# First attention of a two-layer step: score tiles of 768 keys over two PSUM banks, three banks for transposed weights

## The chip, the cores and the metric

One core of a Trainium2 chip runs the whole program. Its engines issue their own instructions in a fixed order: PE (TensorE, matmuls and transposes, with its weight loads listed as PEld), DVE (VectorE), ACT (ScalarE), POOL (GpSimd) and SP (SyncE, which here issues DMAs). The metric is the time of one execution on the device in microseconds; lower is better.

## The reference

One inference step of a backbone of two layers, on 256 prompt tokens and 1024 sample tokens of width 1024, with 512 cached keys for the samples. Layer 0 has a convolution branch and a differential attention; layer 1 has two grouped-query attentions. The attention of layer 0 has 4 heads of two score maps each:

```python
def diff_attend(q, k, v, lam):
    s = jnp.einsum('bqhcd,bkhcd->bhcqk', q, k).astype(F32) * (q.shape[-1] ** -0.5)
    p = jax.nn.softmax(s, axis=-1)
    w = p[:, :, 0] - lam * p[:, :, 1]
    return jnp.einsum('bhqk,bkhv->bqhv', w.astype(v.dtype), v)
```

A sample token attends to 512 cached and 1024 own keys, 1536 in all; a prompt token to the 256 prompt keys. The outcome is normalized, multiplied with a gate, and goes into one output projection together with the convolution branch.

## The kernel before

The kernel keeps float32 results by writing an operand as a high and a low part of a faster 32-bit format. A product is then two or three matmuls that add up in PSUM. PSUM has 8 banks of 128 x 512 float32.

The work of a layer runs in stages: input projection, attention, output projection. In the attention of layer 0, `l0_attn`, the tokens are taken in groups of two row blocks of 128; group 0 is the prompt, groups 1 to 4 the samples. For each of 4 heads and each group, `stage_a` loads the queries (L661, tile `qs`, three of them) and goes through the two row blocks j and the two maps c, with a row of tiles for each pair (j, c):

- Scores: for every 512 keys a PSUM tile `S` takes two matmuls (L777), the high and the low part of the queries in one. A sample row has three such tiles. The pool has three `S` buffers of one bank.
- `row_softmax` (L385 to L398): DVE reads an `S` tile, writes its negative to `E` in SBUF and takes the running minimum into a column of `mm` (L394). The second and third reduce of a row start from the minimum of the one before, so each depends on it. When all of a row is there, ACT takes the exponential of all 1536 columns with its sum (L397).
- After both maps of a block: a reciprocal (L784), a factor (L785), and `E0 += w * E1`, the first 1024 columns on DVE (L787), the last 512 on POOL (L789, L790).

`stage_b` (L668 to L733) then multiplies the weights with the values. For every 256 keys it transposes four blocks of 128 x 128 on PE into a PSUM tile `wt` (L690); four buffers of one bank. That tile is copied out in one of three ways: ACT copies, DVE casts the high part (L371), POOL subtracts for the low part (L372); or ACT does both reads (L374, L375) and POOL subtracts (L376); or ACT copies alone (L696). The products go into the one `pv` bank: three matmuls a chunk (L677 to L679), or one in float32 (L684). At the end of a group ACT copies `pv` out (L710), PE transposes it back into a further `wt` buffer, named `wt_ot` (L717), from which ACT takes squares (L718) and DVE, after a few small steps and a power on POOL (L95), the scaled output `oy` (L724). SP stores it. The tiles of the next stage's first two preparations use `wt` buffers as well.

So the banks are 3 for `S`, 4 for `wt` and 1 for `pv`.

Steps of `stage_b` of one group are put between the rows of the next by a small queue (`BQueue`, L37 to L74) that hands out so many chunks a row. In what order the instructions finally stand on each engine is set by the framework's list scheduler, which the program is opened with (`schedule_with_timeline_sim=True`, L1547); tile pools with their numbers of buffers bound it. On the chip an engine works down its order: behind an instruction that waits, all that follows waits too.

In `phase_attn` (L1274 to L1295) the pools are made, from the numbers in `pb` (L1269). Layer 1 (scores at L1217) shares `row_softmax` and `phase_attn`.

Of the kernel before, what the change touches and what calls it, by code (L numbers as in the profile page):

```python
# [10 lines left out]
F32 = mybir.dt.float32  # L11
# [21 lines left out]
def f32(ap):  # L33
    return ap.bitcast(F32)
# [42 lines left out]
class K:  # L77
# [586 lines left out]
    def l0_attn(self, at, small, pre, sps, wps, pvps, freed, early):  # L664
        nc, a = self.nc, self.a
# [71 lines left out]
        for h in range(4):  # L737
            kd = nxt
            if h == 3:
                freed()  # L740
            nxt = None
            vf = at.tile([128, NT + 4, 128], F32, tag="v", bufs=2, name=f"v{h}")
            nc.sync.dma_start(vf[:, 0:NT], self.V0[h].rearrange("t p c -> p t c"))
            nc.sync.dma_start(vf[:, NT : NT + 4], a["cbv"][h])
            vs = None
            nr = sum(2 for m in self.modes0 if m not in ("a", "d"))
            if nr:
                vs = at.tile([128, 2, nr, 128], F32R, tag="vs", bufs=2, name=f"vs{h}")
                nc.scalar.copy(vs[:, 0], vf[:, 2 : 2 + nr])
                nc.gpsimd.tensor_tensor(vs[:, 1], vf[:, 2 : 2 + nr], f32(vs[:, 0]), ALU.subtract)  # L750
            gzt = at.tile([128, NT, 128], F32, tag="gzt", bufs=2, name=f"gzt{h}")
            nc.sync.dma_start(gzt, self.GZ0[h].rearrange("t p c -> p t c"))

            def stage_a(h, g, kd, vf, vs, gzt):

                tiles = (2 * g, 2 * g + 1)
                sample = g > 0
                kofs = 256 if sample else 0
                nkc = 1536 if sample else 256
                qs = qs1 if (h, g) == (0, 1) else self.l0_query(h, g, at, 3)  # L760
                sc = small.tile([128, 2, 2], F32, tag="sc", bufs=4, name=f"sc{h}_{g}")
                W = []
                for j in range(2):
                    E = []
                    for c in range(2):
                        nmx = f"{h}_{g}_{j}_{c}"
                        q = qs[:, :, c, j * 128 : j * 128 + 128]
                        if sample:
                            e = at.tile([128, 1536], F32, tag=f"E{c}", bufs=(4 if c == 0 else 3), name=f"E{nmx}")
                        else:  # L770
                            e = at.tile([128, 256], F32, tag="Ep", bufs=4, name=f"E{nmx}")
                        parts = []
                        for o in range(0, nkc, 512):
                            n = min(512, nkc - o)
                            S = sps(f"{nmx}_{o}")[:, :n]
                            for hl in range(2):
                                nc.tensor.matmul(S, q[:, hl], kd[:, c, kofs + o : kofs + o + n], start=(hl == 0), stop=(hl == 1))  # L777
                            parts.append((S, o))
                        m = small.tile([128, 4], F32, tag="mm", bufs=8, name=f"mm{nmx}")
                        self.row_softmax(parts, e, sc[:, c, j : j + 1], m)  # L780
                        E.append(e)
                        yield
                    w = small.tile([128, 2], F32, tag="wc", bufs=4, name=f"wc{h}_{g}_{j}")
                    nc.vector.reciprocal(w[:, 0:1], sc[:, 1, j : j + 1])  # L784
                    nc.vector.scalar_tensor_tensor(w[:, 1:2], sc[:, 0, j : j + 1], self.nlam, w[:, 0:1], ALU.mult, ALU.mult)  # L785
                    sp = self.wsp if sample else nkc
                    nc.vector.scalar_tensor_tensor(E[0][:, :sp], E[1][:, :sp], w[:, 1:2], E[0][:, :sp], ALU.mult, ALU.add)  # L787
                    if sp < nkc:
                        nc.gpsimd.tensor_scalar(E[1][:, sp:nkc], E[1][:, sp:nkc], w[:, 1:2], 0.0, ALU.mult, ALU.add)  # L789
                        nc.gpsimd.tensor_tensor(E[0][:, sp:nkc], E[0][:, sp:nkc], E[1][:, sp:nkc], ALU.add)  # L790
                    W.append(E[0])
                bq.put(stage_b(h, tiles, W, sc, nkc // 128, (vf, vs, 2 if sample else 0), gzt), nkc // 256)

            prompt = stage_a(h, 0, kd, vf, vs, gzt)
            for g in range(1, 5):
                for i, _ in enumerate(stage_a(h, g, kd, vf, vs, gzt)):
                    bq.step(4 - i)
                    if (g, i) == (2, 2) and h < 3:
                        nxt = self.l0_keys(h + 1, *((pool, 1) if h == 1 else (at, 2)))
                    if g == self.gp:  # L800
                        next(prompt, None)
                if g == self.gp:
                    for _ in prompt:
                        pass
# [427 lines left out]
def build(tc, a):  # L1232
    nc = tc.nc
    k = K(tc, a)
    with ExitStack() as ctx:
# [30 lines left out]
        def pool(c, name, bufs=1, **kw):  # L1266
            return c.enter_context(tc.tile_pool(name=name, bufs=bufs, **T, **kw))

        pb = (dict(S=3, wt=4), dict(S=3, wt=4))  # L1269

        def right(name):
            return tc.alloc_tile_pool(name=name, bufs=1, side="right", **T)

        def phase_attn(l, fn, pre):  # L1274
            out = []

            def freed():
                while pre[0]:
                    pre[0].pop().release()
                wp = right(f"wop{l}")  # L1280
                out.extend([wp, [k.wo_chunk(l, j, wp) for j in range(k.npre[l])], []])

            def early(t, ps):
                out[2].append(k.prep(l, t, out[0], lambda nm: out[0].tile([128, D], F32, tag="ac2", bufs=1, name=nm), ps))

            with ExitStack() as c:
                at = pool(c, f"at{l}")
                small = pool(c, f"sa{l}", 2)
                psp = pool(c, f"pa{l}", space=PSUM)
                fn(at, small, (pre[0][-1], *pre[1:]),  # L1290
                   lambda nm: psp.tile([128, 512], F32, tag="S", bufs=pb[l]["S"], name=f"S_{nm}"),
                   lambda nm: psp.tile([128, 512], F32, tag="wt", bufs=pb[l]["wt"], name=f"wt_{nm}"),
                   lambda nm: psp.tile([128, 512], F32, tag="pv", bufs=1, name=f"pv_{nm}"),
                   freed, early)
            return out  # L1295
# [13 lines left out]
        with ExitStack() as c1:  # L1309
# [5 lines left out]
            psp = pool(c1, "ps0", space=PSUM)  # L1315
# [85 lines left out]
            k.hlb = 1  # L1401
            k.l0_in(ws, raw, wp, cxp, p1, small, acc, pst, mod, freed0)
        wo = phase_attn(0, k.l0_attn, pre)
        with ExitStack() as c1:
            hpa = pool(c1, "hpa")
            k.use_mod()
            with ExitStack() as c2:
# [13 lines left out]
                psp = pool(c1, "ps1", space=PSUM)  # L1421
# [23 lines left out]
            k.hlb = 2  # L1445
            k.l1_in(ws, (kvw[0], k.nkv), raw, wp, p1, small, acc1, pst1, k.mod_vec(((1, 2),), cr, raw, wp, small, psm1, cst, [k.vec1]), freed1)
        wo = phase_attn(1, k.l1_attn, pre)
        with ExitStack() as c1:
            psp = pool(c1, "ps2", space=PSUM)
# [111 lines left out]
```

## Time and profile before

| | before |
|---|---|
| median of 3 runs | 1828.53 us |
| lowest and highest | 1826.63, 1828.82 us |
| profiled execution, its own time | 1829.44 us |
| its span in the trace | 1827.6 us |
| around the span | 1.84 us |
| mean granted clock of PE | 0.983 |
| PE busy, of the span | 1728.4 us (95%) |
| DVE busy | 1246.9 us (68%) |
| ACT busy | 974.5 us (53%) |
| POOL busy | 780.3 us (43%) |
| first sample reduce of layer 0's attention | at 529.93 us |
| last one | at 783.56 us |

The profiled execution is 0.91 us above the median. Shares of the whole span mix stages with different limits, so the attention of layer 0 is read in windows of its own. In a row of groups, the columns are: line, engine, operation, what is written and read, shapes, the count, then busy time, the mean of one in ns, and the idle time of the engine ahead of these instructions with what ended most of it. In a row of the timeline, they are the start, the duration, engine, line and operation, and in brackets the idle time ahead of it. A reduce at L394 shows up as two records, the reduce and the read of its accumulator.

### The profile page before, as it was taken

The page shows a single profiled execution, that of the slowest core. Times are in us where ns is not written, and L with a number is a line of the kernel's source. Part 1 is how long each engine was busy: PE and PEld are TensorE (multiplying, and loading weights), DVE is VectorE, ACT ScalarE, POOL GpSimd, SP SyncE. Part 2 cuts the span into 40 slices and gives each one's busy share as a digit, 9 for nine tenths or more (in the row PEclk, how much of TensorE's full clock was granted, in tenths as well). Part 3 has the DMA queues.
Part 4 walks back from the last instruction along what each step waited for, and adds up shares of the span by engine and source line. Part 5 has one row for each costly group of instructions (what it writes and reads, how often), then busy time and mean ns, then how long its engine had stood idle before and what let it go on. Part 6 is the DMA issues. An engine that isn't in the chain of part 4 may idle for free. (4 is left out here: it accounts for less than half of the span.)

```text
span 1827.6 us, 28287 instructions
## 1 busy us (share of the span) xinstructions
PE 1728.4 (95%) x9434; PEld 1419.7 (78%) x9434; DVE 1246.9 (68%) x2975; ACT 974.5 (53%) x2040; POOL 780.3 (43%) x696
## 2 busy tenths in 40 slices
PE   6999999999859999899999999998999999999998
PEld 2787888988747777778887778876888888878886
DVE  6657545674779999945576672117999999999322
ACT  6432234444337777653344543217888788898311
POOL 2322022222547787663237873203344344454332
PEclk9999999999969999999999999999999999999999
DMA  8467478785764433144246346254013114141441
GB/s 292 167 164 209 155 189 208 191 225 134 230 192 107 125 104 96 44 140 160 75 158 194 139 122 167 75 137 101 24 41 90 36 38 110 54 146 58 158 171 55
DMA packets 220086, 241.24 MB, mean 132 GB/s; under 512 B 72128, under 2 KB 154464, under 8 KB 219684
## 3 DMA queue, kind: packets, MB, share of 16 engines
q1 hardware_dynamic: 207284, 233.53, 43.2%
q0 software_dynamic: 1792, 3.15, 1.0%
q10 hardware_dynamic: 10864, 2.75, 0.8%
q8 instruction: 75, 1.23, 0.3%
q14 instruction: 71, 0.58, 0.1%
HBM read 169.08 MB, written 70.28 MB: 131 GB/s over the span
## 5 line engine op out<-in xcount | busy, mean ns | idle before, releaser
L397 ACT ACTIVATE E<-E,mm 128x1536 f32<-128x1536 f32 (+3 forms) x240 | 293.2, 1226 | 78.1 <-DVE E L394 63.6
L270 POOL TENSOR_TENSOR w_w<-raw_w,w_w 128x512 fp32r<-128x512 f32 x88 | 118.6, 1358 | 256.2 <-ACT w_w L269 242.4
L1217 PE MATMUL S<-k1d,q1s 128*128 128x512 f32 (+1 forms) x704 | 204.7, 391 | 2.5 <-DVE E L394 0.9
L372 POOL TENSOR_TENSOR el<-ef,eh 128x512 fp32r<-128x512 f32 x96 | 123.9, 1291 | 190.9 <-DVE eh L371 185.9
L394 DVE TENSOR_SCALAR_CACHE_REDUCE E<-S,mm 128x512 f32<-128x512 f32 x256 | 189.8, 743 | 10.7 <-PE S L777 3.7
L1147 PE MATMUL wt_et<-ident,E 128*128 128x128 f32 x1264 | 187.6, 273 | 4.9 <-ACT ef L370 4.4
L1147 PEld LDWEIGHTS wt_et<-ident,E 128*128 128x128 f32 x1264 | 154.7, 140 | 41.3 <-ACT ef L370 4.8
L777 PE MATMUL S<-kd,qs 128*128 128x512 f32 (+1 forms) x416 | 134.2, 433 | 30.4 <-DVE E L394 25.3
L368 DVE TENSOR_TENSOR el<-wt_et,eh 128x512 fp32r<-128x512 f32 x220 | 146.4, 681 | 11.8 <-ACT eh L367 11.3
L1217 PEld LDWEIGHTS S<-k1d,q1s 128*128 128x128 f32 x704 | 119.6, 190 | 27.9 <-DVE E L394 11.8
L1142 PE MATMUL pv_pv<-el,v 128*128 128x512 f32 x316 | 139.3, 441 | 0.4 <-POOL el L372 0.2
L318 PE MATMUL acc_g<-w_w,hi 128*128 128x512 f32 x336 | 131.4, 393 | 1.4 <-DVE v L1000 1.3
L319 PE MATMUL acc_g<-w_w,hi 128*128 128x512 f32 x336 | 132.3, 394 | 0.4 <-POOL w_w L270 0.4
L367 ACT CAST eh<-wt_et 128x512 fp32r<-128x512 f32 x220 | 123.3, 591 | 16.7 <-PE wt_et L1147 16.2
L320 PE MATMUL acc_g<-w_w,lo 128*128 128x512 f32 x336 | 131.6, 392 | 0.0
L1141 PE MATMUL pv_pv<-eh,v 128*128 128x512 f32 x316 | 128.5, 407 | 0.0
L852 PE MATMUL acc_po<-wo,oh 128*128 128x512 f32 x320 | 126.0, 395 | 0.6 <-DVE oy L724 0.6
L853 PE MATMUL acc_po<-wo,oh 128*128 128x512 f32 x320 | 125.1, 392 | 0.0
L394 DVE TENSOR_SCALAR_CACHE_REDUCE E<-S 128x512 f32<-128x512 f32 (+1 forms) x160 | 99.7, 629 | 17.7 <-PE S L1217 9.3
L777 PEld LDWEIGHTS S<-kd,qs 128*128 128x128 f32 x416 | 70.7, 198 | 51.4 <-DVE E L394 38.9
L856 PE MATMUL acc_po<-wo,ol 128*128 128x512 f32 x320 | 103.3, 393 | 0.0
L269 ACT CAST w_w<-raw_w 128x512 fp32r<-128x512 f32 x96 | 59.2, 621 | 79.4 <-DMA raw_w<-in_wod 21.2
(294 smaller groups left out, 4555.4 us busy)
## 6 DMA issues: line engine op xcount, KB each, us to landing
rawm_v<-in_wmodt SPq DMA_DIRECT2D x64, 256.0 KB, 3.1
raw_w<-in_we SPq DMA_DIRECT2D x56, 256.0 KB, 3.4
X<-AW SPq DMA_DIRECT2D x32, 336.0 KB, 5.6
qs<-QK SPq DMA_DIRECT2D x80, 128.0 KB, 2.9
ac<-CAT SPq DMA_DIRECT2D x20, 512.0 KB, 4.3
raw_w<-in_wod SPq DMA_DIRECT2D x40, 256.0 KB, 2.8
q1s<-qT SPq DMA_DIRECT2D x40, 256.0 KB, 2.6
xraw_m<-in_wmod SPq DMA_DIRECT2D x32, 256.0 KB, 5.2
```

The lines of the kernel that those rows point to most:

```text
L318: nc.tensor.matmul(ps[:, o:], a, w[:, 0, o:], start=(k == 0), stop=False)
L319: nc.tensor.matmul(ps[:, o:], a, w[:, 1, o:], start=False, stop=False)
L320: nc.tensor.matmul(ps[:, o:], b, w[:, 0, o:], start=False, stop=(k == KC - 1))
L368: nc.vector.tensor_tensor(lo, ps, f32(hi), ALU.subtract)
L394: nc.vector.tensor_scalar(e[:, o : o + w], S, -1.0, init, ALU.mult, ALU.min, accum_out=m[:, i : i + 1])
L397: nc.scalar.activation(e[:, :n], e[:, :n], AF.Exp, bias=init, scale=-1.0, accum_out=s)
L777: nc.tensor.matmul(S, q[:, hl], kd[:, c, kofs + o : kofs + o + n], start=(hl == 0), stop=(hl == 1))
L852: nc.tensor.matmul(po[hn], oh[:, k, :], wo[k][:, 0, s], start=(k == 0), stop=False)
L1141: nc.tensor.matmul(pv, vs, wh, start=(i == 0), stop=False)
L1142: nc.tensor.matmul(pv, vs, wl, start=False, stop=(i == nk - 1))
L1147: nc.tensor.transpose(ps[:, g * 128 : g * 128 + 128], E[g][:, ec : ec + 128], self.ident)
L1217: nc.tensor.matmul(S, qs[:, g, :], kd[hl][:, kc : kc + n], start=(hl == 0), stop=(hl == 1))
```

## The change

In layer 0 an `S` tile has two banks ([128, 1024] float32), of which 768 columns are used, and there are two such buffers. A sample row of 1536 keys is two tiles. Each is filled by four matmuls, two of 512 columns in its first bank and two of 256 in its second, and read by one reduce of 768 columns. A prompt row (256 keys) is one tile with two matmuls of 256, as it was, in a buffer of two banks. The `wt` pool has three buffers. So the banks are 4 + 3 + 1. Layer 1 has the numbers that it had. From L777 on, lines stand three further down (the score matmul is L780, L784 becomes L787, L787 becomes L790).

```diff
-                        for o in range(0, nkc, 512):
-                            n = min(512, nkc - o)
+                        for o in range(0, nkc, 768):
+                            n = min(768, nkc - o)
                             S = sps(f"{nmx}_{o}")[:, :n]
-                            for hl in range(2):
-                                nc.tensor.matmul(S, q[:, hl], kd[:, c, kofs + o : kofs + o + n], start=(hl == 0), stop=(hl == 1))
+                            for b in range(0, n, 512):
+                                w = min(512, n - b)
+                                ko = kofs + o + b
+                                for hl in range(2):
+                                    nc.tensor.matmul(S[:, b : b + w], q[:, hl], kd[:, c, ko : ko + w], start=(hl == 0), stop=(hl == 1))
                             parts.append((S, o))
...
-        pb = (dict(S=3, wt=4), dict(S=3, wt=4))
+        pb = (dict(S=2, sw=1024, wt=3), dict(S=3, sw=512, wt=4))
...
-                   lambda nm: psp.tile([128, 512], F32, tag="S", bufs=pb[l]["S"], name=f"S_{nm}"),
+                   lambda nm: psp.tile([128, pb[l]["sw"]], F32, tag="S", bufs=pb[l]["S"], name=f"S_{nm}"),
```

Since the scheduler sets the order anew, instructions also move. They do so in the attention of layer 0 alone; ahead of it and behind it every engine has the order that it had. In the names, `S_3_1_0_512` is the score tile of group 3, block 1, map 0, from key 512 on, `wt_wt_4_2` the transposed weights of group 2 (blocks 4 and 5) from chunk 2 on, and the last number counts tiles.

DVE, head 0, in the second half of group 3's rows, before:

```order
L394 TENSOR_SCALAR E_3_1_0_5890,mm_3_1_0_5900<-S_3_1_0_512_5894,mm_3_1_0_5900 128x512
L724 SCALAR_TENSOR_TENSOR oy_2_5867<-wt_ot_2_5857,oss_2_5858,gzt_5501 128x128 x2
L371 CAST wh_4_4_5852<-wf_4_4_5851 128x512
L394 TENSOR_SCALAR E_3_1_0_5890,mm_3_1_0_5900<-S_3_1_0_1024_5897,mm_3_1_0_5900 128x512
L394 TENSOR_SCALAR E_3_1_1_5931,mm_3_1_1_5941<-S_3_1_1_0_5932 128x512
L784 RECIPROCAL wc_3_0_5884<-sc_3_5784 128x1
L394 TENSOR_SCALAR E_3_1_1_5931,mm_3_1_1_5941<-S_3_1_1_512_5935,mm_3_1_1_5941 128x512
L785 SCALAR_TENSOR_TENSOR wc_3_0_5884<-sc_3_5784,ls,wc_3_0_5884 128x1
L394 TENSOR_SCALAR E_3_1_1_5931,mm_3_1_1_5941<-S_3_1_1_1024_5938,mm_3_1_1_5941 128x512
L787 SCALAR_TENSOR_TENSOR E_3_0_0_5785<-E_3_0_1_5831,wc_3_0_5884,E_3_0_0_5785 128x1024
```

The same place after:

```order
L394 TENSOR_SCALAR E_3_1_0_5890,mm_3_1_0_5901<-S_3_1_0_768_5896,mm_3_1_0_5901 128x768
L724 SCALAR_TENSOR_TENSOR oy_2_5867<-wt_ot_2_5857,oss_2_5858,gzt_5501 128x128 x2
L787 RECIPROCAL wc_3_0_5884<-sc_3_5784 128x1
L788 SCALAR_TENSOR_TENSOR wc_3_0_5884<-sc_3_5784,ls,wc_3_0_5884 128x1
L790 SCALAR_TENSOR_TENSOR E_3_0_0_5785<-E_3_0_1_5831,wc_3_0_5884,E_3_0_0_5785 128x1024
L394 TENSOR_SCALAR E_3_1_1_5931,mm_3_1_1_5942<-S_3_1_1_0_5932 128x768
L394 TENSOR_SCALAR E_3_1_1_5931,mm_3_1_1_5942<-S_3_1_1_768_5937,mm_3_1_1_5942 128x768
L394 TENSOR_SCALAR E_4_0_0_5974,mm_4_0_0_5985<-S_4_0_0_0_5975 128x768
```

The row (3, 1, 1) has two reduces for three, and they stand directly behind one another, with the next row's first reduce behind them; before, small instructions stood between. The update of E0 (L787, now L790) has moved from behind this row to ahead of it.

PE, at the output's transposes of group 1 (`wt_ot_2`) and the weights of group 2, before:

```order
L777 MATMUL S_3_0_1_1024_5838<-kd_5145,qs_3_5779 128x512 x2
L717 MATMUL wt_ot_2_5857<-ident,oT_2_5800 128x128
L777 MATMUL S_3_1_0_0_5891<-kd_5145,qs_3_5779 128x512 x2
...
L690 MATMUL wt_wt_4_0_5802<-ident,E_2_1_0_5685 128x128
...
L690 MATMUL wt_wt_4_2_5820<-ident,E_2_1_0_5685 128x128
...
L690 MATMUL wt_wt_4_4_5846<-ident,E_2_1_0_5685 128x128
...
L777 MATMUL S_3_1_0_512_5894<-kd_5145,qs_3_5779 128x512 x2
L690 MATMUL wt_wt_4_6_5871<-ident,E_2_0_0_5582 128x128
```

And after:

```order
L690 MATMUL wt_wt_4_4_5846<-ident,E_2_1_0_5685 128x128
...
L717 MATMUL wt_ot_2_5857<-ident,oT_2_5800 128x128
L690 MATMUL wt_wt_4_6_5871<-ident,E_2_0_0_5582 128x128
...
L780 MATMUL S_3_0_1_768_5837<-kd_5145,qs_3_5779 128x512 x2
L780 MATMUL S_3_0_1_768_5837<-kd_5145,qs_3_5779 128x256 x2
L677 MATMUL pv_pv_4_5801<-wh_4_0_5808,vs_5498 128x256
L690 MATMUL wt_wt_4_8_5905<-ident,E_2_0_0_5582 128x128
...
L717 MATMUL wt_ot_2_5857<-ident,oT_2_5800 128x128
L780 MATMUL S_3_1_0_0_5891<-kd_5145,qs_3_5779 128x512 x2
L780 MATMUL S_3_1_0_0_5891<-kd_5145,qs_3_5779 128x256 x2
```

Before, the output's tile is opened while three tiles of weights are open (their first transposes stand a little ahead of these rows, their others behind it): four in all. After, those three are finished first and the output's tile is opened behind them; between its two transposes stand two tiles of weights, one score tile and a product.

## The prediction

> **What bounds the kernel now.** I read the page's busy slices first, to place the changed stage, and then the same stretch by windows, by groups and by waits.
>
> ```profile
> PE   6999999999859999899999999998999999999998
> DVE  6657545674779999945576672117999999999322
> 545.00:765.00 220.00, 203.44 (x1146) 164.21 (x1144) 207.64 (x548) 163.23 (x327) 163.90 (x130) 0.98 0.37 103
> ```
>
> A slice is 45.7 us. VectorE (DVE) stands at 9 in slices 13 to 17, the attention of layer 0, while in most of the other slices only PE does. The window row (PE, PEld, DVE, ACT, POOL busy, then the clock 0.98) covers the steady part of that stage: DVE is idle 220 − 207.64 = 12.4 us and PE 16.6 us. So both are nearly full. Which one leads is seen in the groups of 530 to 780 us, and in the waits of 545 to 765 us (total, times, longest):
>
> ```profile
> L777 PE MATMUL S<-kd,qs 128*128 128x512 f32 x374 | 124.3, 441 | 30.2 <-DVE E L394 25.1 <-DMA qs<-QK 4.6
> L394 DVE TENSOR_SCALAR_CACHE_REDUCE E<-S,mm 128x512 f32<-128x512 f32 x125 | 92.7, 744 | 7.4 <-PE S L777 3.7
> L394 DVE TENSOR_SCALAR_CACHE_REDUCE E<-S 128x512 f32<-128x512 f32 x63 | 43.0, 682 | 5.1 <-PE S L777 4.7 <-PE wt_wt L690 0.3
> L690 PE MATMUL wt_wt<-ident,E 128*128 128x128 f32 x368 | 55.9, 282 | 7.4 <-DVE E L787 5.5 <-ACT E L397 1.0 <-POOL E L790 0.7
> L696 ACT COPY wf<-wt_wt 128x512 f32<-128x512 f32 x46 | 26.4, 595 | 2.9 <-PE wt_wt L690 2.3 <-POOL wl L376 0.4 <-POOL wl L372 0.2
> ```
> ```profile
> PEld S L777 <- DVE E L394: 18.2, 38, 1.3
> DVE E L394 <- PE S L777: 6.6, 10, 1.4
> PE S L777 <- DVE E L394: 6.3, 13, 1.0
> ```
>
> The score matmul (L777) and its weight load wait for a reduce that has to free an S bank, 51 times for 24.5 us. The reduce waits for scores only 10 times, for 6.6 us. DVE leads and PE follows closely. And the transposes (L690) never wait for an eviction: four wt banks are enough today.
>
> **The change part by part.** *Fewer, longer reduces.* What a reduce costs is its start to the next start, since the accumulator read runs beside the next instruction:
>
> ```profile
> 611.09 0.40 DVE L394 TENSOR_SCALAR_CACHE_REDUCE E<-S 128x256 f32<-128x256 f32 x1
> 611.42 0.08 DVE L394 DVE_READ_ACCUMULATOR E<-S 128x1 f32 x1
> ...
> 612.87 0.68 DVE L394 TENSOR_SCALAR_CACHE_REDUCE E<-S 128x512 f32<-128x512 f32 x1
> 613.48 0.08 DVE L394 DVE_READ_ACCUMULATOR E<-S 128x1 f32 x1
> 613.69 0.75 DVE L394 TENSOR_SCALAR_CACHE_REDUCE E<-S,mm 128x512 f32<-128x512 f32 x1
> 614.37 0.09 DVE L394 DVE_READ_ACCUMULATOR E<-S,mm 128x1 f32 x1
> 614.58 0.75 DVE L394 TENSOR_SCALAR_CACHE_REDUCE E<-S,mm 128x512 f32<-128x512 f32 x1
> ```
>
> A row's first reduce holds DVE 0.61 us (612.87 to 613.48), one that takes a running minimum 0.68 (613.69 to 614.37), and one of 256 columns 0.33 (611.09 to 611.42). So 256 columns more are worth 0.61 − 0.33 = 0.28, and reduces of 768 columns should hold 0.89 and 0.96. A row of 1536 keys costs 0.61 + 2 × 0.68 = 1.97 before and 0.89 + 0.96 = 1.85 after: 0.12 us less. There are 4 heads × 4 sample groups × 2 tiles × 2 maps = 64 such rows: −7.7 us. No row reads across a bank's edge. If the edge cost a whole start again, 256 columns would cost 0.33, not 0.28, twice a row, 0.10 of the 0.12, and nothing much would be left. A row that is longer for no reason but its length gives the first value, which I take.
>
> A second reduce that stands directly behind the first of its own row waits for its minimum: 613.48 to 613.69 and 614.37 to 614.58 are 0.21 us of nothing. In DVE's order 31 pairs stand so before and 18 after: 13 × 0.21 = −2.7 us. Together −10.4 us, on DVE, which leads.
>
> In its section "Optimizing Scalar/DVE Operations" the page "Perfetto Trace Analysis" of the Trainium skill says that grouping into larger operations helps if the engine is saturated, and that breaking them up can help where an unsaturated engine makes bubbles on others. The window bears out its first half for this stage (DVE busy 207.64 of 220); by it the whole saving would count, as in the first rival. The second half would speak for the old tiles, since PE does wait for DVE here.
>
> *More matmuls.* 64 rows have 4 matmuls of 512 and 4 of 256 columns instead of 6 of 512; 128 more weight loads with them.
>
> ```profile
> 635.34 0.28 PE L678 MATMUL pv_pv<-wl,vs 128*128 128x256 f32 x1
> 635.46 0.28 PE L679 MATMUL pv_pv<-wh,vs 128*128 128x256 f32 x1
> 635.58 0.28 PE L677 MATMUL pv_pv<-wh,vs 128*128 128x256 f32 x1
> ...
> 636.05 0.62 PE L777 MATMUL S<-kd,qs 128*128 128x512 f32 x2
> 636.51 0.28 PE L678 MATMUL pv_pv<-wl,vs 128*128 128x256 f32 x1
> ```
>
> Each product of 256 columns has its own weights and still follows the last by 0.12 us; two of 512 take 0.46 (636.05 to 636.51). So 4 × 0.12 replaces 2 × 0.23: PE pays about 0.02 a row, 1 us in all, which its 16.6 us of idle time hide. Without that cover it would be +1 us.
>
> *Two score buffers for three.* A freed buffer is filled by PE and read by DVE:
>
> ```profile
> 635.54 0.75 DVE L394 TENSOR_SCALAR_CACHE_REDUCE E<-S,mm 128x512 f32<-128x512 f32 x1 [0.42 <-PE S L777]
> 636.22 0.08 DVE L394 DVE_READ_ACCUMULATOR E<-S,mm 128x1 f32 x1
> 636.71 0.75 DVE L394 TENSOR_SCALAR_CACHE_REDUCE E<-S,mm 128x512 f32<-128x512 f32 x1 [0.41 <-PE S L777]
> ```
>
> The two matmuls from 636.05 serve the reduce at 636.71: the second starts 0.23 in, so a reduce follows the start of its last matmul by 0.43. For 768 columns the last of four matmuls starts 0.23 + 0.23 + 0.12 = 0.58 after the first; with about 0.1 from release to start a buffer is back after 1.1 us. Meanwhile DVE has one queued tile, 0.89 to 0.96 us, where it had two of 0.61 to 0.68 against a return of 0.1 + 0.23 + 0.43 = 0.76. So each place where two or more tiles stand in DVE's order with too little between loses what is missing of 1.1 us. Summing durations of the rows above along the order, I find 21 such places among 142 with 4.3 us missing, against 3 with 0.3: +4.0 us. That assumes a PE that is free at once. With PE in the middle of other work each place loses more (the 0.42 us above are such waits); at half a microsecond for each of the 21, +10 us. The low end is nothing, if PE's fills move ahead in the order by as much. I take +4.0, because the waits of DVE on S that the row shows are short (0.66 us mean).
>
> The first sample group doesn't gain all of its share, because the next one waits for its queries:
>
> ```profile
> 542.58 2.50 PE L777 MATMUL S<-kd,qs 128*128 128x512 f32 x4 [4.60 <-DMA qs<-QK]
> 544.27 0.69 DVE L394 TENSOR_SCALAR_CACHE_REDUCE E<-S 128x512 f32<-128x512 f32 x1 [2.54 <-PE S L777]
> ```
>
> Four rows' share and three of the pairs lie ahead of this: 4 × 0.12 + 3 × 0.21 = +1.1 us given back. Later query loads are issued a group ahead, three tiles deep; the longest wait on scores after 545 us is 1.4 us. SP's order swaps some query loads with output stores, for which I count nothing, by that cover.
>
> *Three banks for transposed weights.* One of the banks is often held by the output's transposes:
>
> ```profile
> 590.87 0.68 DVE L394 TENSOR_SCALAR_CACHE_REDUCE E<-S 128x512 f32<-128x512 f32 x1
> ...
> 656.39 0.68 DVE L394 TENSOR_SCALAR_CACHE_REDUCE E<-S 128x512 f32<-128x512 f32 x1
> ...
> 725.30 0.33 PE L717 MATMUL wt_ot<-ident,oT 128*128 128x128 f32 x1
> 730.52 0.27 PE L717 MATMUL wt_ot<-ident,oT 128*128 128x128 f32 x1
> ...
> 737.51 0.61 DVE L724 SCALAR_TENSOR_TENSOR oy<-wt_ot,oss,gzt 128x128 f32<-128x128 f32 x2
> ```
>
> From the first transpose to the last read it holds the bank 12.8 us, of the 16.4 us that a group takes (a quarter of the time between the first sample reduces of heads 1 and 2, at 590.87 and 656.39). So two banks remain for E's transposes, each cycle four transposes and a copy of 0.6 us (L696) that may stand behind an exp of 1.6 us. PE issues in order: behind a transpose that waits stand the score matmuls, and DVE waits for those. Following each tile from its first transpose to its last eviction in the trace, 51 of 124 began while three others were held. At a mean 1.3 us each that is 65 us of waits that don't exist today. The bounds are 0 (PE has 16.6 us to spare, and the new order puts the transposes later, with products between) and +20, if a third of it reaches DVE through the one queued tile. I take +1.5: the order was made with three banks, and the transposes' present waits (7.4 us of PE) are all for E, which will come sooner.
>
> The sum: −7.7 − 2.7 + 4.0 + 1.1 + 1.5 = −3.8 us. All else runs in the old order behind the stage and only moves up. The profiled execution takes 1829.44 us (span 1827.6), 0.91 over the median of 1828.53; 1829.4 − 3.8 = 1825.6, and beside the median, 0.9 lower, **1824.7**, which I say.
>
> **The rivals.** *The whole gain.* The fills keep ahead, since order and buffers fit: −10.4 + 1.1 = −9.3, some 1819 to 1820. For it: DVE is busy 94%, and its waits on S are 6.6 us now. Against it: one queued tile instead of two.
>
> *PSUM runs out (slower).* Transposes wait for a third bank, and the reduces behind them for scores. If a quarter of the 65 us reaches DVE, +16: 1829.4 − 10.4 + 5.1 + 16 = 1840. It decides from 65 × 0.14 = 9 us on, where the total passes +3.7 us. For it: the bank held 12.8 us and PE's 92%. Against it: today's transposes wait for none.
>
> "Optimization Strategy" on the same page of the Trainium skill takes a gap that repeats on the engine that should be full as a sign that there may not be PSUM enough for the next tile. The 51 waits of L777 on L394 are such gaps on PE at present; after the change the same rule would point at L690's waits on evictions.
>
> *No change.* Either the edge of a bank costs a start again, or PE's fills of twice the grain give the saving back: −10.4 + 10 (the 21 places at half a microsecond each) + 1.1 + 1.5 = +2.2, or with the edge 64 × 0.10 = 6.4 dearer, −3.8 + 6.4 = +2.6: 1826 to 1832. For it: PE is the next engine by only 4 us of idle time.
>
> **How the numbers follow.** What a measurement here can tell from no change is about 0.2%, 3.7 us: below 1824.9 is faster, above 1832.2 slower. The forecast (1822 to 1828) has 0.37, the whole gain 0.17, no change 0.20, PSUM running out 0.26. The forecast's own values lie on both sides of 1824.9, two thirds of the chance below. So: faster 0.17 + 0.25 = 0.42; slower 0.26 + 0.02 = 0.28; the same 0.30. The range takes in the whole gain with a little below it and most of the slower case: 1817 to 1839.
>
> **What would show it.** Right: 128 reduces of 768 columns at 0.89 to 0.96 us start to start in place of 192; DVE's busy time lower by 8 to 10 us; DVE waiting for S more often than 10 times, for about 11 us in the steady part; PE's waits for L394 shorter. The wt step is right if L690 waits for evictions by a few microseconds at most; wrong, and the slower rival right, if those waits are over 15 us and DVE's waits on S grow with them. Reduces of over 1.0 us start to start would show a price of the bank's edge. The rest of the program, from the output projection on, should keep its length; a difference there would make the whole argument wrong.

## The result and the profile after

The change makes the kernel slower: 1847.73 us (median of 4 runs, 1847.08 to 1848.25) against 1828.67 (4 runs), a ratio of 1.0099 with a 95% interval of 1.0080 to 1.0118. The forecast was 1824.7, with a range up to 1839.

The span of the profiled execution grew from 1827.6 to 1846.4 us. Of these 18.8 us, 14.3 lie in the stage from the first to the last reduce of layer 0's attention. The windows of that stage, of the kernel before and of the changed one (PE, PEld, DVE, ACT, POOL busy):

```profile
529.93:784.31 254.38, 231.59 (x1277) 186.24 (x1278) 237.28 (x634) 186.04 (x366) 182.82 (x145) 0.96 0.39 106
```
```profile
533.53:802.23 268.70, 234.11 (x1397) 201.68 (x1397) 241.23 (x507) 186.15 (x367) 182.39 (x145) 0.96 0.37 100
```

DVE is busy 3.9 us more, where 10 less were due, and idle 27.5 us instead of 17.1. The output projection's first matmul follows the last reduce after 17.3 us instead of 16.7, and the rest is as long as before (1026.8 and 1026.6 us). Another 3.6 us lie ahead of the stage, where the order is the same. In the profiles of all kernels below the stage starts anywhere from 529.7 to 537.8 us, so I don't count them as the change's; where they come from is open.

The reduces do what was worked out. These are the first of the changed kernel's timeline (start, duration):

```profile
533.53 0.95 DVE L394 TENSOR_SCALAR_CACHE_REDUCE E<-S 128x768 f32<-128x768 f32 x1
534.40 0.08 DVE L394 DVE_READ_ACCUMULATOR E<-S 128x1 f32 x1
534.61 1.02 DVE L394 TENSOR_SCALAR_CACHE_REDUCE E<-S,mm 128x768 f32<-128x768 f32 x1
535.55 0.08 DVE L394 DVE_READ_ACCUMULATOR E<-S,mm 128x1 f32 x1
```

A row's two reduces hold DVE 0.87 and 0.94 us, 1.81 for the 1.97 of before: 64 x 0.16 = 10 us saved (9 on the mean of all the stage's rows), and the edge between two banks costs nothing. What took them back is in DVE's other instructions and in its waits. The groups of the stage, before and after (busy, mean ns):

```profile
L787 DVE SCALAR_TENSOR_TENSOR E<-E,wc,E 128x1024 f32<-128x1024 f32 x30 | 43.5, 1451 | 0.3
L785 DVE SCALAR_TENSOR_TENSOR wc<-sc,ls,wc 128x1 f32<-128x1 f32 x39 | 14.4, 377 | 0.4
L719 DVE SCALAR_TENSOR_TENSOR oss<-sc 128x2 f32<-128x2 f32 x19 | 8.1, 426 | 0.0
L720 DVE SCALAR_TENSOR_TENSOR oss<-oss 128x2 f32<-128x2 f32 x18 | 5.9, 328 | 0.0
```
```profile
L790 DVE SCALAR_TENSOR_TENSOR E<-E,wc,E 128x1024 f32<-128x1024 f32 x31 | 48.6, 1569 | 0.4
L788 DVE SCALAR_TENSOR_TENSOR wc<-sc,ls,wc 128x1 f32<-128x1 f32 x39 | 18.5, 476 | 0.6
L719 DVE SCALAR_TENSOR_TENSOR oss<-sc 128x2 f32<-128x2 f32 x19 | 9.4, 496 | 0.0
L720 DVE SCALAR_TENSOR_TENSOR oss<-oss 128x2 f32<-128x2 f32 x18 | 12.2, 676 | 0.0
```

The instructions are the same, and all four kinds got longer. The program has 32, 40, 20 and 20 of them (a few records are missing), so, at the mean of those on record, they cost 3.8 + 4.0 + 1.4 + 7.0 = 16.2 us more. With the other kinds (the casts of L371, the 8 updates of 256 columns, the reciprocals and L724) all of DVE's instructions but the reduces take 137.3 us for 125.3, worked out in the same way: +12.0. DVE's waits, before and after:

```profile
DVE E L394 <- PE S L777: 9.8, 12, 2.5
DVE wc L784 <- ACT E L397: 1.6, 5, 0.6
```
```profile
DVE E L394 <- PE S L780: 14.5, 23, 2.0
DVE wc L787 <- ACT E L397: 6.5, 8, 1.4
DVE oy L724 <- POOL oss L95: 1.7, 3, 1.1
DVE wh L371 <- ACT wf L370: 0.9, 4, 0.3
DVE E L394 <- PE wt_wt L690: 0.6, 1, 0.6
```

In sum 24.2 us for 12.6: +11.6. So −10 for the reduces, +12.0 and +11.6, with 0.7 left over, make the stage's +14.3. The fit is better than the method: added up in the same way for the kernels below, the terms miss the stage by −5 (e10) to +8 us (e14). PE's waits for a bank of transposed weights are hardly among the causes; for matmuls this one is all there is, and their weight loads wait 0.6 us:

```profile
PE wt_wt L690 <- ACT wf L375: 0.2, 1, 0.2
```

Why does an instruction of one column take up to 1.33 us? In the changed kernel's timeline one L788 starts as a POOL instruction ends and the next begins, and it ends with that one. L790 behind it begins with the third POOL instruction and outlasts it by 1.1 us. DVE first, then POOL (start, duration):

```profile
559.85 1.33 DVE L788 SCALAR_TENSOR_TENSOR wc<-sc,ls,wc 128x1 f32<-128x1 f32 x1
561.21 2.83 DVE L790 SCALAR_TENSOR_TENSOR E<-E,wc,E 128x1024 f32<-128x1024 f32 x1
```
```profile
558.62 1.28 POOL L376 TENSOR_TENSOR wl<-wf,wh 128x512 fp32r<-128x512 f32 x1
559.87 1.29 POOL L372 TENSOR_TENSOR wl<-wf,wh 128x512 fp32r<-128x512 f32 x1
561.12 1.84 POOL L750 TENSOR_TENSOR vs<-v,vs 128x768 fp32r<-128x768 f32 x1
562.95 1.66 POOL L792 TENSOR_SCALAR E<-E,wc 128x512 f32<-128x512 f32 x1
```

L788 runs to 561.18, POOL's L372 to 561.16. Over the stage an L788 without POOL beside it takes 0.22 us (20 of them), one with POOL beside more than half of it 0.89 (15); before, 0.22 (21) and 0.64 (15). The changed kernel's stage has 18 records of L788 or L720 that last over 0.6 us, the longest 3.44, and each of them ends within 0.03 us of the end of a POOL instruction. Reduces and reciprocals, which have one tensor input, don't care: with POOL beside them or not, the first reduce of a row takes 0.95 us, the second 1.01 and a reciprocal 0.16. But one input is no safeguard: the casts of L371, from SBUF to SBUF, take 0.42 us without POOL (10 of them) and 0.70 with it (20). And L724, which has one of its two tensors in PSUM, takes 0.34 on the mean in both kernels. The page "Perfetto Trace Analysis" of the Trainium skill says in "Optimizing Scalar/DVE Operations" that GpSimd and VectorE share a read port of SBUF. These rows agree for instructions with both tensors in SBUF, and for the casts.

My theory after this comparison was "POOL beside DVE": the new order puts DVE's instructions with two tensors in SBUF (two-input instructions, below) beside POOL's. The rivals were "two buffers" (DVE and PE wait for each other) and "banks" (the third wt bank). The experiments call the first one "order" as well.

### The profile page after: what moved, and what is told of

Same layout as the page of the kernel before. It is cut to its first block, busy times and chain, and to the rows that moved or that the text cites. A ratio compares the mean times of both kernels' runs of the same rounds, so it can differ in the third digit from the quotient of the medians.

```text
span 1846.4 us, 28380 instructions
## 1 busy us (share of the span) xinstructions
PE 1735.2 (94%) x9562; PEld 1437.9 (78%) x9562; DVE 1245.8 (67%) x2847; ACT 974.2 (53%) x2040; POOL 780.2 (42%) x696
## 5 line engine op out<-in xcount | busy, mean ns | idle before, releaser
L372 POOL TENSOR_TENSOR el<-ef,eh 128x512 fp32r<-128x512 f32 x96 | 124.0, 1291 | 191.4 <-DVE eh L371 187.4
L394 DVE TENSOR_SCALAR_CACHE_REDUCE E<-S,mm 128x512 f32<-128x512 f32 (+1 forms) x192 | 159.6, 832 | 10.8 <-PE S L780 5.6
L780 PE MATMUL S<-kd,qs 128*128 128x256 f32 (+1 forms) x544 | 131.2, 369 | 33.7 <-DVE E L394 29.2
L780 PEld LDWEIGHTS S<-kd,qs 128*128 128x128 f32 x544 | 96.3, 199 | 57.1 <-DVE E L394 38.5
L367 ACT CAST eh<-wt_et 128x512 fp32r<-128x512 f32 x220 | 123.5, 592 | 16.2 <-PE wt_et L1150 15.6
L394 DVE TENSOR_SCALAR_CACHE_REDUCE E<-S 128x768 f32<-128x768 f32 (+2 forms) x160 | 117.0, 735 | 21.5 <-PE S L1220 9.3
```

The source lines that it names most:

```text
L394: nc.vector.tensor_scalar(e[:, o : o + w], S, -1.0, init, ALU.mult, ALU.min, accum_out=m[:, i : i + 1])
L780: nc.tensor.matmul(S[:, b : b + w], q[:, hl], kd[:, c, ko : ko + w], start=(hl == 0), stop=(hl == 1))
```

## The experiments

All ratios are to the kernel before on the same chip, with 95% intervals. Each edit also makes the scheduler set the order anew. "Others" is the time of DVE's instructions but the reduces in the stage, worked out as above (in e9 and e10 without the small instruction that they add). At the least durations in these traces (1.27 us for an update of 1024 columns, 0.22 for a factor, 0.42 for a cast, and so on) others would be some 92 us, an estimate; the instructions that were longer than that in the rows above had POOL's work beside them.

Two cautions for the table. The profile shows one execution, and not the median one: e2's was the slowest of ten, e11's the fastest. And the time that lies neither in the stage nor between its last reduce and the output projection, where no edit changes an instruction, is anywhere from 1556 to 1567 us in these profiles. So a ratio within some 0.5% of another may owe its difference to that, and the stage has to be looked at too.

| kernel | ratio | stage, us | others, us | DVE's waits, us |
|---|---|---|---|---|
| before | 1 | 254.4 | 125.3 | 12.6 |
| changed | 1.0099 | 268.7 | 137.3 | 24.2 |
| e1: three wt banks | 1.0099 | 265.0 | 133.5 | 14.7 |
| e2: four S of 512, three wt | 1.0034 | 255.4 | 130.5 | 12.0 |
| e3: two S of 512 | 1.0191 | 287.9 | 125.9 | 38.4 |
| e4: changed, factor by tensor_scalar | 1.0070 | 262.2 | 128.7 | 27.4 |
| e5: three wt, one for wt_ot | 1.0080 | 263.6 | 129.7 | 18.4 |
| e6: before, factor by tensor_scalar | 1.0025 | 256.8 | 127.8 | 12.6 |
| e7: changed, no POOL combination | 0.9940 | 244.3 | 110.6 | 24.6 |
| e8: before, no POOL combination | 0.9933 | 244.8 | 113.9 | 14.3 |
| e9: changed, POOL's part later | 1.0061 | 265.1 | 129.7 | 25.3 |
| e10: before, POOL's part later | 1.0013 | 255.3 | 132.0 | 5.7 |
| e11: changed, L792 on ACT | 1.0019 | 255.3 | 132.4 | 17.6 |
| e12: before, L789 on ACT | 1.0040 | 254.2 | 122.2 | 14.3 |
| e13: e1, no POOL combination | 0.9956 | 246.0 | 115.1 | 13.2 |
| e14: e3, no POOL combination | 1.0118 | 276.3 | 114.9 | 36.9 |
| e15: changed, e4 and e11 | 1.0008 | 248.4 | 119.2 | 25.5 |

**e1, the third wt bank alone.**

```diff
-        pb = (dict(S=3, wt=4), dict(S=3, wt=4))
+        pb = (dict(S=3, wt=3), dict(S=3, wt=4))
```

> The kernel before with three wt banks in layer 0 instead of four, one bank unused; score tiles stay three of 512 keys. Theory 'banks' (the loss of 19 us comes from the third wt bank): 1840 to 1848 us. Theory 'two buffers' (it comes from two score buffers of twice the grain): 1826 to 1831. Theory 'order' (it comes from DVE's two-input instructions that the new order puts beside POOL's): anything, but the time over 1828.6 goes with the time of L785, L787, L719 and L720, which was 72 us in the kernel before and 85 in the changed one.

1849.48 us, 1.0099 (1.0070 to 1.0128). "Banks" had the size, and this edit has no wide tile in it. But the stage lost its 10.6 us where the third theory looked: others +8.2, waits +2.1. The four groups that the expectation names come to 78 us, between 72 before and the changed kernel's 89 (by the rows above; the expectation's 85 is too low). PE's matmuls wait 2.2 us for a bank of weights (L690 on L696), which is not nothing but far from 10.6. DVE's busy time in the stage rose by 7.5 us, to 244.8, for the same instructions (the stage's window, then two groups):

```profile
531.76:796.72 264.96, 233.55 (x1277) 183.24 (x1278) 244.78 (x633) 184.90 (x364) 183.31 (x144) 0.98 0.38 101
```
```profile
L787 DVE SCALAR_TENSOR_TENSOR E<-E,wc,E 128x1024 f32<-128x1024 f32 x30 | 45.8, 1527 | 0.2
L720 DVE SCALAR_TENSOR_TENSOR oss<-oss 128x2 f32<-128x2 f32 x17 | 9.1, 536 | 0.0
```

**e2, four small score buffers and three wt banks.**

```diff
+        pb = (dict(S=4, wt=3), dict(S=3, wt=4))
```

> Score tiles of 512 keys as before, but four buffers, and three wt banks: the banks are divided as in the changed kernel (4 + 3 + 1), only the tiles are small. 'Banks': 1840 to 1848. 'Two buffers': 1824 to 1829, since four small buffers lack nothing. 'Order': as in the run above, with the time of DVE's two-input instructions.

1839.82 us, 1.0034 (1.0022 to 1.0047), between the two expectations. With the same three banks a fourth score buffer wins back two thirds of e1's loss: its stage is as long as before, and 4.8 us are lost at its end (the output projection starts 21.5 us after the last reduce, not 16.7). As a division of the same eight banks, four small score tiles are better than two wide ones by 0.65%.

**e3, two score buffers of 512 keys.**

```diff
+        pb = (dict(S=2, wt=4), dict(S=3, wt=4))
```

> Two score buffers of one bank (512 keys), four wt banks, nothing else changed. 'Two buffers': 1838 to 1850, as bad as the changed kernel or worse, because the queued tile is even shorter (0.68 us against a return of 0.76), with DVE waiting for scores more than 12 times and over 15 us. 'Banks': 1827 to 1832. 'Order': with the time of the two-input instructions.

1867.37 us, 1.0191 (1.0168 to 1.0214), beyond the top of what "two buffers" expected. Here it is waits, and others don't move (+0.6):

```profile
DVE E L394 <- PE S L777: 27.4, 32, 3.4
```

All of DVE's waits are 25.8 us up, of the stage's 33.5. So there are two losses that look different in the profile: fewer score buffers make waits, fewer wt banks make others longer.

**e4 and e6, the factor by an instruction of one tensor input**, in the changed kernel and in the one before:

```diff
-                    nc.vector.scalar_tensor_tensor(w[:, 1:2], sc[:, 0, j : j + 1], self.nlam, w[:, 0:1], ALU.mult, ALU.mult)
+                    nc.vector.tensor_scalar(w[:, 1:2], sc[:, 0, j : j + 1], self.nlam, w[:, 0:1], ALU.mult, ALU.mult)
```

> The changed kernel with one instruction in another form: the factor w1 (39 in the stage, L788) is made by tensor_scalar with one tensor input instead of scalar_tensor_tensor with two. If DVE's two-input instructions are what POOL holds up ('order'), these take 0.2 us each instead of 0.48, 10 us less of DVE: 1837 to 1843. If they are held up for another reason (waiting for an operand), they stay at 0.4 to 0.5 us and the time at 1845 to 1849. 'Two buffers' and 'banks' alone expect 1844 to 1848.

> The kernel before with the factor w1 (L785) made by tensor_scalar instead of scalar_tensor_tensor. 'Order' (POOL holds up DVE's two-input instructions in both kernels): L785 at 0.25 instead of 0.38 us, 40 x 0.13 = 5 us of DVE, 0.997 to 0.999 of before. If DVE doesn't lead in the stage: 0.999 to 1.001.

In the changed kernel 1844.10 us, 1.0070 (1.0055 to 1.0085). By its microseconds this is just outside what "order" expected; the kernel before takes 1832.17 on this chip, 3.5 more than when the expectation was worked out, and by the ratio it lies inside (1.0046 to 1.0078). L788 comes down from 476 to 269 ns:

```profile
L788 DVE TENSOR_SCALAR wc<-sc,ls,wc 128x1 f32<-128x1 f32 x39 | 10.4, 269 | 0.6
```

That is 8.3 us of DVE for a stage shorter by 6.5. With one tensor input the instruction isn't held up: each takes 0.26 to 0.28 us, beside POOL or not. In the kernel before the expectation failed: 1.0025 (1.0009 to 1.0041), slower. L785 does come down to 270 ns, but in the new order L787 rises from 1451 to 1546 and L719 from 426 to 574, so others are 2.5 us longer and so is the stage. So a change of the order that nobody intended can be worth some 0.3%.

**e5, a bank of its own for the output's transposes.**

```diff
+        pb = (dict(S=3, wt=3), dict(S=3, wt=4))
...
+                   lambda nm: psp.tile([128, 512], F32, tag="ot" if l == 0 and nm.startswith("ot") else "wt", bufs=1 if l == 0 and nm.startswith("ot") else pb[l]["wt"], name=f"wt_{nm}"),
```

> The kernel before with its four wt banks divided: three for transposed weights and one of its own for the output's transposes (wt_ot). Three banks shared by both cost 1.0% in an earlier run. Theory 'held bank' (the output's tile holds one of three banks for most of a group, so two remain): most of that loss is gone, 1.000 to 1.004 of before. Theory 'four open tiles' (the transposes themselves need four banks at times): 1.006 to 1.010.

1846.89 us, 1.0080 (1.0053 to 1.0107). The idea of the prediction that the output's tile leaves only two banks falls: with three for the weights alone the loss stays. What is left of the two theories is that the order makes use of a fourth open tile of weights. That isn't shown by itself: others are 4.4 us up here and waits 5.8, another mixture than in e1.

**e7 and e8, without POOL's part of the combination**, the changed kernel and the one before. L792 and L793 (L789 and L790) are left out, so the last 512 keys keep the first map's weights.

```diff
-                    if sp < nkc:
-                        nc.gpsimd.tensor_scalar(E[1][:, sp:nkc], E[1][:, sp:nkc], w[:, 1:2], 0.0, ALU.mult, ALU.add)
-                        nc.gpsimd.tensor_tensor(E[0][:, sp:nkc], E[0][:, sp:nkc], E[1][:, sp:nkc], ALU.add)
```

> The changed kernel without POOL's part of the weights' combination (L792, L793 left out: the last 512 keys keep their first map's weights). 60 of POOL's 130 instructions in the steady part go. To be compared with the next run. 'Order' (the wide kernel loses to POOL beside DVE): the ratio of this to the next comes down from 1.010 to 1.000 to 1.004. 'Banks' or 'two buffers': it stays at 1.007 to 1.012, with DVE's waits for scores still at 14 us.

> The kernel before without POOL's part of the combination, as in the run above. DVE's two-input instructions lose 10 to 20 us in each kernel: 0.990 to 0.997 of before.

0.9940 (0.9917 to 0.9964) and 0.9933 (0.9906 to 0.9959). The gap of 1.0% is gone: 0.07%, with some 0.4% of uncertainty either way. The two stages are equally long, and the windows and DVE's waits show why (wide, then narrow):

```profile
530.45:774.79 244.34, 226.74 (x1393) 198.37 (x1393) 216.94 (x507) 185.45 (x366) 101.85 (x84) 0.96 0.41 110
```
```profile
DVE E L394 <- PE S L780: 15.6, 25, 2.3
DVE wc L787 <- ACT E L397: 5.6, 10, 1.6
```
```profile
530.50:775.33 244.83, 223.60 (x1274) 182.17 (x1275) 226.45 (x633) 185.58 (x367) 101.75 (x84) 0.98 0.41 109
```
```profile
DVE E L394 <- PE S L777: 8.4, 10, 2.9
DVE wc L784 <- ACT E L397: 1.9, 5, 0.7
```

The wide kernel's DVE is busy 9.5 us less, as its reduces should make it, and it waits 10.3 us more. That part of "two buffers" is right: without POOL's part, the two cancel. POOL still does its other work, and others are above 92 us in both.

**e9 and e10, POOL's part after DVE's.** A small instruction of one input reads a column that L790 (before: L787) wrote, and hands POOL the factor (the tile `w` gets a third column for it):

```diff
+                        nc.vector.tensor_scalar(w[:, 2:3], E[0][:, 0:1], 0.0, w[:, 1:2], ALU.mult, ALU.add)
-                        nc.gpsimd.tensor_scalar(E[1][:, sp:nkc], E[1][:, sp:nkc], w[:, 1:2], 0.0, ALU.mult, ALU.add)
+                        nc.gpsimd.tensor_scalar(E[1][:, sp:nkc], E[1][:, sp:nkc], w[:, 2:3], 0.0, ALU.mult, ALU.add)
```

> The changed kernel with POOL's part of each combination (L792, L793) made to start after DVE's part (L790) instead of with it: a small DVE instruction of one input, which reads a column of L790's output, hands POOL the factor. Theory 'POOL beside DVE': L790 comes down from 1.57 to 1.3 us, 32 x 0.27 = 9 us of DVE less 32 x 0.2 = 6 for the small instruction, and L788, L719 and L720 change with the order; 1.002 to 1.008 of before instead of 1.010. Theory 'two buffers': no change or worse, 1.009 to 1.013, because POOL's part is ready later.

> The same edit in the kernel before. 'POOL beside DVE': 32 x (1.45 - 1.3) = 5 us gained and 6 paid: 0.998 to 1.002.

1.0061 (1.0042 to 1.0079) and 1.0013 (0.9994 to 1.0032). In the changed kernel L790 falls from 1569 to 1407 ns and others by 7.6 us (the small instruction not counted). The stage falls by 3.6 and the time by 0.4%; the waits stay. In the kernel before it is another matter: others rise by 6.7 us, the small instruction adds some 6.5, waits fall by 6.9, and the stage is only 0.9 longer. So more of others is not a loss by itself; the waits can give way to it.

**e11 and e12, a part of POOL's work on ACT.**

```diff
-                        nc.gpsimd.tensor_scalar(E[1][:, sp:nkc], E[1][:, sp:nkc], w[:, 1:2], 0.0, ALU.mult, ALU.add)
+                        nc.scalar.activation(E[1][:, sp:nkc], E[1][:, sp:nkc], AF.Copy, scale=w[:, 1:2])
```

> The changed kernel with L792 (E1 times the factor, 512 columns) on ACT instead of POOL, so that POOL works 37 us less in the stage and ACT some 20 more. 'POOL beside DVE': DVE's instructions other than reduces take 6 to 12 us less than the 137 of the changed kernel; 1.002 to 1.007 of before. 'Two buffers': 1.008 to 1.013, and ACT's longer queue delays exps.

> The same edit in the kernel before. 'POOL beside DVE': DVE's other instructions take some 6 us less than 125, so 0.996 to 1.000 of before, if ACT's further 20 us hold nothing up.

1.0019 (1.0004 to 1.0034) for the wide kernel, at the lower edge of what was expected, and 1.0040 (1.0023 to 1.0057) for the narrow one, which was to gain. Others fell by 4.9 us in the wide one, where 6 to 12 were expected, and waits by 6.6. In the narrow one others fell by 3.1, but its stage is as long as before: 254.2 us, against 255.3 in the wide one. So the wide kernel is the faster one here by some 0.2%, but not by its stage: the profiles differ ahead of it and behind it, which is open.

**e13 and e14, the two single losses without POOL's part.** The edits of e1 and e3 with that of e7, which leaves the same part out.

> Small score tiles, three buffers, three wt banks (1.010 of before as it was), now without POOL's part of the combination (the last 512 keys keep their first map's weights). The same without that part but with four wt banks took 0.993. If the third bank costs its 1.0% by way of POOL and DVE: 0.992 to 0.997. If it costs by transposes that wait for a bank: 1.001 to 1.005.

> Two score buffers of 512 keys, four wt banks (1.019 of before as it was), without POOL's part of the combination, which is left out as in the run above. Two buffers cost by waits between PE and DVE, which POOL has no part in: 1.008 to 1.015, DVE's waits for scores still over 20 us. If POOL carries this loss too: 0.993 to 0.999.

0.9956 (0.9939 to 0.9973): beside e8's 0.9933 the third bank now costs 0.2%, of its 1.0%, with some 0.3% of uncertainty either way. And 1.0118 (1.0091 to 1.0145): beside e8, two small score buffers still cost 1.85% of their 1.9%, by waits:

```profile
DVE E L394 <- PE S L777: 30.9, 39, 2.1
```

This tells the two apart: most of the loss of the bank goes away with POOL's part, the loss of a score buffer does not.

**e15, both edits that helped the changed kernel** (e4 and e11).

> The changed kernel with both edits that helped it: L792 on ACT (1.002 of before) and the factor by tensor_scalar (0.3% less). 'POOL beside DVE': DVE's other instructions below 125 us, 0.996 to 1.000 of before. If what these edits moved was only the order, anything from 0.998 to 1.006.

1.0008 (0.9988 to 1.0027): no gain over the kernel before that could be measured. Others are below 125 us, as "POOL beside DVE" had it, but the ratio is just above its range and inside that of the rival, that these edits only moved the order. The stage is shorter by 6 us (248.4), but the output projection starts 23.6 us after its last reduce instead of 16.7. No kernel that computes everything beat the one before.

## Why the prediction was wrong

- *Fewer reduces, −7.7.* Right, and a little small: −9 to −10. The rival price of a bank's edge (a reduce of over 1.0 us start to start) is excluded: 0.94.
- *Dependent pairs, −2.7.* Right in number: the trace has 32 of them before and 18 after. DVE's idle time that no wait explains went from 17.1 − 12.6 = 4.5 to 27.5 − 24.2 = 3.3 us, −1.2; the read of the accumulator fills 0.08 us of each pause.
- *More matmuls, hidden.* PE is busy 2.5 us more in the stage, and nothing points to it as a cost.
- *Two score buffers, +4.0.* Right for what it counted, +4.7 on scores (18 waits of 11.7 us in the steady part, from 548.6 to 782.9, where about 11 were forecast), but a part wasn't in it: +4.9 on exps. A reciprocal that the new order puts ahead of the next row's reduces waits for the row's exp, and the reduces wait behind it. The upper bound of 10 holds for the waits on scores, but not for all of DVE's, which are 11.6 up, and 10.3 without POOL's part. PE's waits for the reduces were to get shorter and got longer, 30.6 us for 24.5 in the steady part.
- *The first group gives back 1.1.* Right in kind: from its first reduce to the second group's, 14.16 us for 14.34, so it kept 0.2.
- *Three banks, +1.5.* The step "two banks remain for E's transposes ... behind a transpose that waits stand the score matmuls" failed. PE's matmuls waited 0.2 us for evictions, and a bank of its own for the output's tile (e5) helps little. Yet the bank alone costs as much as the whole change (e1). Most of that goes with POOL's combination (e13).
- *What the sum lacked, the step that turned a gain into a loss.* It took every other DVE instruction at the duration of before, a term put at nothing without a reason. They were 12.0 us longer in the new order, more than the reduces saved, so DVE was busy 3.9 us more and not 8 to 10 less. The rows for this stood in the trace of before: L785 of one column takes 377 ns on the mean and 0.22 us when POOL is idle.
- *The slower rival*, PSUM running out (0.26), had the sign and over half of the size (1840 is 11 us above the profiled execution of before, the measured one 19), but not the mechanism: its point of decision, 9 us of waits for banks that reach DVE, was not reached. The rule of the page "Perfetto Trace Analysis" of the Trainium skill, section "Optimization Strategy", that stood beside it would have had L690 wait for evictions; the trace has 0.2 us of such gaps.

The sum with the measured sizes: −10 for reduces, +11.6 for waits, +12.0 for others, 0.7 left over. Shown, within the 0.3 to 0.4% that these pairs leave open, is that the wide tiles' gain and the two buffers' waits cancel (e7 against e8) and that the rest of the loss goes away with POOL's combination (the same pair, and e1 against e13). Shown by the rows and e4 is that instructions with two inputs in SBUF are longer beside POOL. That they are the whole way by which POOL's part costs is argued from the size of others, 8 us in e1 and 12 in the changed kernel; e10 and e12, where others moved and the stage hardly did, speak against a simple sum. Taking POOL's part away also makes the weights ready sooner, and no run holds the order fixed to tell these two apart. It is open too why an order made for three banks puts more of DVE's work beside POOL's.

## What to carry to other kernels

Where an order is made anew, durations of before are no constants: look for groups whose mean is far above their minimum, find what ran beside them, and take their least and greatest as bounds of a term of their own. A bank taken from a pool may cost 1% with next to no waits for it in the profile (0.2 us here, 2.2 in e1), because the order is built around it; try it alone first. And a saving on the leading engine that takes away a buffer must be set against all of that engine's waits, not just those on the buffer.

## What was not expected of the hardware

A DVE instruction of one column that reads two tensors in SBUF took 0.22 us alone and up to 1.33 beside POOL, ending with POOL's instruction; with one tensor input it took 0.27 on the mean at the same place (e4). One of two columns (L720) took 0.15 alone and once 3.44, to the end of the fourth of four POOL instructions (two of them DMA issues). A reduce over 768 columns of two banks went on over the edge at the same pace per column.
